# A hybrid two-layer block: the low parts of the second MLP product's weights made by an accumulating transfer

## The chip, the cores and the metric

The kernel runs on one core of one Trainium2 chip. The metric is the device time of one execution in microseconds; three runs of the kernel before gave 2245.93, 2249.05 and 2250.21, and their median, 2249.05, is the time before. A profile is one further execution.

## The reference

Two layers over 512 latent tokens and 256 context tokens, width 1024, in float32. Each layer normalizes and modulates, makes one input projection for three mixers (neighbourhood attention, a bidirectional linear recurrence, windowed attention), merges and projects them, and then runs an MLP with a squared ReLU. Only the MLP matters here:

```python
def sq_relu_mlp(h, w1, w2):
    return jnp.square(jax.nn.relu(h @ w1)) @ w2

# per layer, latent tokens; context tokens the same in layer 0
h2 = modulate(rms_norm(x, norm2_g[l]), mod_l[3], mod_l[4])
x = x + mod_l[5] * sq_relu_mlp(h2, w_ff1[l], w_ff2[l])
# at the end
return rms_norm(x, final_g)
```

`w_ff1` is 1024 x 4096 and `w_ff2` 4096 x 1024 in each layer.

## The kernel before

**Products in three passes.** Every large product is made with operands split in two float32r parts, `x = xh + xl`, `w = wh + wl`. TensorE multiplies wh by xh, wl by xh and wh by xl, in this order (`PASSES`, `gemm1`, L382), for each of the 128-row steps. So `wl` is needed at the second matmul of a weight.

**Weights.** A list `wseq` holds all weight chunks in the order of use. A chunk is 128 x 1024 float32, 512 KB. `w_load` issues its transfer from DRAM into a tile `wr` on SP's queue (L276). `w_split` then makes `wh` by a copy to float32r on ScalarE (L290) and `wl` by `raw - wh` on VectorE (L291). `w_get` hands the pair to the product; `w_ahead` writes loads and splits for some eight tiles ahead of use. All these tiles, also the raw ones and those of the modulation weights (`mw`), rotate through one pool of 12 slots (`whp`). A tile gets a slot when the last reader of an older one is done, and the instruction that first writes it waits for that.

**The MLP.** Each layer has 8 blocks of the second product. A block uses four chunks `("w2", l, n, j)`, each for two groups of 128 output rows. The first product's pairs (`("p", n)`) and the second's blocks (`("F", n)`) alternate: two pairs, then a block; the last two blocks follow each other. From pair 3 (layer 0) or 4 (layer 1) on, the first product is made with seven smaller products in place of eight (`seven`, L1507), whose weight forms `wf` are made on ScalarE (L311) and VectorE (L305 to L312) from two raw chunks. In `seven` ScalarE copies a result out of PSUM (`sv`, L1516, L1526) and VectorE adds or subtracts it (L1519, L1529, L1532) before TensorE goes on with the same PSUM tile. In layer 0 both latent and context tokens run (512 and 256 columns), and the results of the first seven blocks are scaled by ScalarE into `xo` (L1641) and added in DRAM to `xsp` by an accumulating transfer on POOL's queue (L1643), eight a block. In layer 1 only the latent tokens are left, and VectorE adds the results to `x` (L1384). During layer 0's MLP the modulation of layer 1 is made on VectorE from 48 chunks `mw` (L521, L536, L541).

**What sets the order.** The order of instructions on each engine is set when the program is built, by priorities and a scheduler's own estimate of times; `hp("ws")` shifts the priority of the split. Each engine then runs its queue strictly in that order. POOL does little: constants, 16 additions, the reciprocal square roots of the norms (L609) and the 56 transfers of L1643. Tiles are named by kind and number; `wh393` and `wl393` are the parts of the first chunk of layer 1's second-to-last block, `wh98` those of the first chunk of layer 0's second block. A number behind that (`wh393_21181`) is a count of tiles and differs between programs.

Of the kernel before, what the change touches and what calls it, by code (L numbers as in the profile page):

```python
# [8 lines left out]
F32R = mybir.dt.float32r  # L9
BF16 = mybir.dt.bfloat16  # L10
AF = mybir.ActivationFunctionType
ALU = mybir.AluOpType
# [53 lines left out]
def f(ap):  # L66
    return ap.bitcast(F32)
# [66 lines left out]
def build(tc, A, out):  # L134
    nc = tc.nc

    with ExitStack() as es:
# [46 lines left out]
        act = nc.scalar.activation  # L184

        def hp(tag):
            return tc.high_priority(HPS[tag]) if HPS.get(tag) else ExitStack()
# [41 lines left out]
        wseq = []  # L229
# [23 lines left out]
        ws = dict(load=0, split=0, use=0)  # L253
        wraw = {}
        whl = {}
        wpart = {}

        def w_tile(name, n, dt):
            return whp.tile([P, 1024], dt, tag="wh", name=f"{name}{n}")

        def w_load(i):
            while ws["load"] <= min(i, len(wseq) - 1):
                n = ws["load"]
                if wseq[n][0] == "f1":
                    _, l, p_, j = wseq[n]
                    if j == 0:
                        for c in range(2):
                            fraw[c] = w_tile("wr%d" % c, n, F32)
                            nc.sync.dma_start(fraw[c], A["w_ff1"][l, 2 * p_ + c])
                    ws["load"] += 1  # L270
                    continue
                a = A[src[wseq[n][0]]]
                for ix in wseq[n][1:]:
                    a = a[ix]
                wraw[n] = w_tile("wr", n, F32)[:, 0:a.shape[1]]
                nc.sync.dma_start(wraw[n], a)  # L276
                ws["load"] += 1

        def w_split(i):
            while ws["split"] <= min(i, len(wseq) - 1):  # L280
                n = ws["split"]
                w_load(n)
                if wseq[n][0] == "f1":
                    whl[n] = form(n, wseq[n][3])
                    ws["split"] += 1
                    continue
                r = wraw.pop(n)
                h_, l_ = (w_tile(nm, n, F32R)[:, 0:r.shape[1]] for nm in ("wh", "wl"))
                with hp("ws"):
                    act(h_, r, AF.Copy)  # L290
                    V.tensor_tensor(l_, r, f(h_), op=ALU.subtract)  # L291
                whl[n] = (h_, l_)
                ws["split"] += 1
# [4 lines left out]
        def form(n, j):  # L298

            a, b, c, d = (fraw[i // 2][:, 512 * (i % 2):512 * (i % 2) + 512] for i in range(4))  # L300
            t = w_tile("wf", n, F32R)
            with hp("ws"):
                if j == 1:
                    s1 = fraw[2] = t3("s1")[:, 0:512]
                    V.tensor_tensor(s1, c, d, op=ALU.add)  # L305
                    V.tensor_tensor(c, c, a, op=ALU.add)
                    V.tensor_tensor(a, a, s1, op=ALU.add)  # L307
                if j == 5:
                    V.tensor_tensor(b, b, a, op=ALU.add)
                r = (a, a, b, fraw.get(2), c, b, d)[j]  # L310
                act(t[:, 0:512], r, AF.Copy)  # L311
                V.tensor_tensor(t[:, 512:1024], r, f(t[:, 0:512]), op=ALU.subtract)  # L312
                if j == 3:
                    fraw.pop(2)
                if j == 6:
                    fraw.clear()
            return t
# [579 lines left out]
        for l in range(L):  # L897
# [648 lines left out]
            for it, n_ in ff_order():  # L1546
# [111 lines left out]
                a = held = None  # L1658
# [114 lines left out]
```

## Time and profile before

| what | us |
|---|---|
| median of three runs | 2249.05 |
| the profiled execution, its own time | 2246.54 |
| its span (first to last instruction) | 2244.7 |
| TensorE busy with matmuls | 2200.5 (98%) |
| VectorE busy | 1533.8 (68%) |
| ScalarE busy | 1190.4 (53%) |
| POOL busy | 91.6 (4%) |

The granted clock is 0.997 of full speed over the span. The span and 1.8 us around it make the execution's time. Matmuls overlap, so the duration of one says little; the distance between the starts of two that follow each other is what one costs. In the views, PE is TensorE, PEld its weight loads, DVE VectorE, ACT ScalarE, POOL GpSimd, SP the engine that issues most transfers; a name with q (SPq) is that engine's sequencer. L382 is line 382. Layer 0's blocks of the second product lie between 837 and 1310 us, layer 1's between 1918 and 2234 us.

### The profile page before, as it was taken

How to read it: one execution, taken by the hardware profiler on the slowest of the kernel's cores; microseconds unless marked ns; L12 is line 12 of the kernel's file. 1: busy time of each engine (PE TensorE's matmuls, PEld its weight loads, DVE VectorE, ACT ScalarE, POOL GpSimd, SP SyncE). 2: the span in 40 equal slices, each digit the busy share in tenths (PEclk: the TensorE clock that was granted, in tenths of full speed). 3: DMA queues.
4: the chain of work that ended last, by engine and by line, in shares of the span. 5: the costliest groups of instructions: out<-in, count | busy, mean ns of one | idle time of the engine just before them, and what ended most of it. 6: DMA issues, size and time to landing. Idle time of an engine off the chain costs nothing.

```text
span 2244.7 us, 35216 instructions
## 1 busy us (share of the span) xinstructions
PE 2200.5 (98%) x13617; PEld 1918.4 (85%) x13617; DVE 1533.8 (68%) x3313; ACT 1190.4 (53%) x2267; POOL 91.6 (4%) x86
## 2 busy tenths in 40 slices
PE   9999999999999999999999999999999999999998
PEld 6888888888888888998889887888878789888997
DVE  5867545677698895766666378654477777777776
ACT  4666446667532274454545446655575845444452
POOL 0000000001000001111000100000000100000000
PEclk9999999999999999999999999999999999999999
DMA  7201121112255536766776732112112232323331
GB/s 280 76 29 43 44 76 43 34 55 78 69 176 188 199 111 145 176 168 178 202 210 162 180 129 76 57 63 73 41 62 89 89 132 86 110 78 94 113 104 66
DMA packets 84502, 246.02 MB, mean 110 GB/s; under 512 B 9824, under 2 KB 13168, under 8 KB 84336
## 3 DMA queue, kind: packets, MB, share of 16 engines
q1 hardware_dynamic: 75840, 221.62, 29.5%
q0 software_dynamic: 8064, 22.02, 6.3%
q8 instruction: 107, 1.75, 0.3%
q14 instruction: 59, 0.48, 0.1%
q10 hardware_dynamic: 432, 0.14, 0.0%
HBM read 212.28 MB, written 30.42 MB: 108 GB/s over the span
## 4 chain that ended last, share of the span: by engine, by line
PE 77%; DVE 10%; ACT 7%; DMA 5%; issue 2%; POOL 0%; SPq 0%; DVEq 0%; POOLq 0%; ACTq 0%
PE gl L382 29%; PE S L382 21%; PE gc L382 5%; PE S L1507 4%; PE S L724 3%; PE O L742 3%; PE gl L1507 3%; PE gl L397 2%; DMA wr<-in_w_ff_dram 2%; PE S L672 2%; DVE wf L312 1%; PE S L673 1%; DMA mw<-in_w_mod_dram 1%; DVE wl L291 1%; PE S L397 1%
## 5 line engine op out<-in xcount | busy, mean ns | idle before, releaser
L291 DVE TENSOR_TENSOR wl<-wr,wh 128x1024 fp32r<-128x1024 f32 (+1 forms) x224 | 269.3, 1203 | 144.9 <-ACT wh L290 79.7
L290 ACT ACTIVATE wh<-wr 128x1024 fp32r<-128x1024 f32 (+1 forms) x224 | 231.6, 1038 | 93.0 <-DMA wr<-in_w_in_dram 45.7
L382 PE MATMUL gl<-hh,wh 128*128 128x512 f32 (+1 forms) x672 | 257.9, 384 | 4.7 <-DVE KL L941 2.1
L382 PE MATMUL gl<-hh,wl 128*128 128x512 f32 (+1 forms) x672 | 255.4, 380 | 0.0
L382 PE MATMUL gl<-hl,wh 128*128 128x512 f32 (+1 forms) x672 | 254.7, 379 | 0.0
L311 ACT ACTIVATE wf<-wr 128x512 fp32r<-128x512 f32 x150 | 90.2, 624 | 145.6 <-DVE wr L307 75.3
L382 PEld LDWEIGHTS gl<-hh,wh 128*128 128x128 f32 x672 | 127.0, 189 | 25.9 <-issue 5.0
L382 PEld LDWEIGHTS gl<-hl,wh 128*128 128x128 f32 x672 | 126.9, 189 | 23.8
L382 PEld LDWEIGHTS gl<-hh,wl 128*128 128x128 f32 x672 | 126.9, 189 | 18.8
L700 ACT ACTIVATE P<-S,s 128x512 f32<-128x512 f32 (+1 forms) x160 | 103.0, 647 | 70.8 <-DVE s L696 35.5
L312 DVE TENSOR_TENSOR wf<-wr,wf 128x512 fp32r<-128x512 f32 x150 | 100.9, 688 | 56.3 <-ACT wf L311 55.8
L382 PE MATMUL S<-ah,wh 128*128 128x512 f32 (+1 forms) x384 | 136.4, 355 | 0.0
L382 PE MATMUL S<-al,wh 128*128 128x512 f32 (+1 forms) x384 | 136.4, 355 | 0.0
L382 PE MATMUL S<-ah,wl 128*128 128x512 f32 (+1 forms) x384 | 136.3, 355 | 0.0
L382 PE MATMUL S<-hh,wl 128*128 128x512 f32 (+1 forms) x360 | 125.1, 348 | 1.1 <-DVE wl L291 1.1
L382 PE MATMUL gl<-ah,wl 128*128 128x512 f32 (+1 forms) x352 | 124.8, 355 | 0.2 <-DVE wl L291 0.2
L382 PE MATMUL S<-hl,wh 128*128 128x512 f32 (+1 forms) x360 | 124.7, 347 | 0.0
L382 PE MATMUL S<-hh,wh 128*128 128x512 f32 (+1 forms) x360 | 124.5, 346 | 0.2 <-ACT tau L1222 0.2
L382 PE MATMUL gl<-al,wh 128*128 128x512 f32 (+1 forms) x352 | 124.6, 354 | 0.0
L382 PE MATMUL gl<-ah,wh 128*128 128x512 f32 (+1 forms) x352 | 124.5, 354 | 0.0
L727 ACT ACTIVATE P<-S 128x512 f32<-128x512 f32 (+1 forms) x160 | 84.4, 554 | 61.6 <-PE S L724 56.7
L1507 PE MATMUL S<-hh,wf 128*128 128x384 f32 (+1 forms) x488 | 109.3, 313 | 5.4 <-ACT sv L1516 3.3
(412 smaller groups left out, 5943.7 us busy)
## 6 DMA issues: line engine op xcount, KB each, us to landing
wr<-in_w_ff_dram SPq DMA_DIRECT2D x128, 512.0 KB
wr<-in_w_in_dram SPq DMA_DIRECT2D x100, 512.0 KB
mw<-in_w_mod_dram SPq DMA_DIRECT2D x48, 512.0 KB
xsp<-xo POOLq DMA_DIRECT2D x56, 384.0 KB, 5.8
mr<-in_w_mod_dram SPq DMA_DIRECT2D x64, 256.0 KB
wr<-in_w_branch_dram SPq DMA_DIRECT2D x24, 512.0 KB
wm<-in_w_mod_dram SPq DMA_DIRECT2D x32, 256.0 KB
wr<-in_w_out_dram SPq DMA_DIRECT2D x16, 512.0 KB
```

The lines of the kernel that those rows point to most:

```text
L290: act(h_, r, AF.Copy)
L291: V.tensor_tensor(l_, r, f(h_), op=ALU.subtract)
L311: act(t[:, 0:512], r, AF.Copy)
L312: V.tensor_tensor(t[:, 512:1024], r, f(t[:, 0:512]), op=ALU.subtract)
L382: mm(o, w[wi_][:, c0 + k * P:c0 + (k + 1) * P], view(acts[k][xi]), start=(k == 0 and i == 0), stop=(k == n - 1 and i == 2))
L397: mm(os_[i], w[wi_][:, k * P:(k + 1) * P], seg.nat(acts[k][xi]), start=(k == 0 and p_ == 0), stop=(k == n - 1 and p_ == 2))
L672: mm(d, qs[:, qc:qc + P], rk, start=True, stop=False)
L700: act(p[:, 0:n0], self.S[i][:, 0:n0], AF.Exp, bias=nm[:, i:i + 1], accum_out=su[:, i:i + 1])
L724: nc.tensor.transpose(d, self.p[i][:, j * P:(j + 1) * P], ident)
L727: act(pt[:, 0:n0], self.S[i][:, 0:n0], AF.Copy)
L742: mm(o[half, oc:oc + P], vt[:, vc:vc + 64], h["pt"][:, j * P:(j + 1) * P], start=(j == 0), stop=(j == nt - 1), tile_position=(0, 64 * h["h ...
L1507: mm(o, w[:, c0:c0 + P], B[i, k][xi], start=(first and k == 0 and n == 0), stop=(last and k == 3 and n == 2), skip_group_check=True)
```

## The change

The chunks of the second product (`w2`, 64 in all) are split in another way. `w_load` takes two tiles, `wh` and `wl`, and issues a transfer on POOL's queue that goes from the float32 chunk in DRAM straight into `wh`, which is float32r: the transfer casts. `w_split` then lets ScalarE write `-wh` into `wl`, and issues a second transfer on POOL's queue that adds the float32 chunk from DRAM to `wl` (`accum_op=ALU.add`), so that `wl = raw - wh`. No raw tile is used, and no VectorE instruction. All other weights stay as they are.

```diff
@@ w_load
+                if wseq[n][0] == "w2":
+                    wraw[n] = tuple(w_tile(nm, n, F32R) for nm in ("wh", "wl"))
+                    nc.gpsimd.dma_start(wraw[n][0], a)
+                    ws["load"] += 1
+                    continue
                 wraw[n] = w_tile("wr", n, F32)[:, 0:a.shape[1]]
                 nc.sync.dma_start(wraw[n], a)
                 ws["load"] += 1
@@ w_split
+                if wseq[n][0] == "w2":
+                    h_, l_ = whl[n] = wraw.pop(n)
+                    with hp("ws"):
+                        act(l_, f(h_), AF.Copy, scale=-1.0)
+                    nc.gpsimd.dma_start(l_, A["w_ff2"][wseq[n][1:]], accum_op=ALU.add)
+                    ws["split"] += 1
+                    continue
                 r = wraw.pop(n)
```

In the changed program lines below the edit have moved on by 12 (L382 is L394, L1643 is L1655); the new transfers are L277 and L296, the negation is L295.

POOL, from the last addition into `xsp` of layer 0's first block to the first of its second block. Before, its queue holds only these additions:

```order
L1643 DMA xsp_109<-xo_1017_8821 128x768
L1643 DMA xsp_109<-xo_1020_8851 128x768
L1643 DMA xsp_109<-xo_1049_9184 128x768
L1643 DMA xsp_109<-xo_1052_9218 128x768
L1643 DMA xsp_109<-xo_1056_9263 128x768
```

Now, in the same place:

```order
L1655 DMA xsp_109<-xo_1020_8847 128x768
L277 DMA wh98_9042<-in_w_ff2_dram 128x1024
L277 DMA wh99_9077<-in_w_ff2_dram 128x1024
L296 DMA wl98_9043<-in_w_ff2_dram 128x1024
L277 DMA wh100_9109<-in_w_ff2_dram 128x1024
L296 DMA wl99_9078<-in_w_ff2_dram 128x1024
L277 DMA wh101_9157<-in_w_ff2_dram 128x1024
L296 DMA wl100_9110<-in_w_ff2_dram 128x1024
L296 DMA wl101_9158<-in_w_ff2_dram 128x1024
L1655 DMA xsp_109<-xo_1049_9176 128x768
```

Eight transfers stand between the additions of two blocks, loads and accumulations in turn, with two loads ahead of the first accumulation.

ScalarE, at the split of that block's first two chunks. Before:

```order
L642 ACTIVATE ah_1035_9017<-r_1025_8879 128x768
L1516 ACTIVATE sv_1041_9026<-S_1037_9022 128x384
L1522 ACTIVATE r_1039_9024<-S_1037_9022 128x384
L290 ACTIVATE wh98_9048<-wr98_9046 128x1024
L1526 ACTIVATE sv_1041_9026<-gl_1042_9080 128x384
L290 ACTIVATE wh99_9084<-wr99_9082 128x1024
```

Now:

```order
L654 ACTIVATE ah_1035_9013<-r_1025_8875 128x768
L1528 ACTIVATE sv_1041_9022<-S_1037_9018 128x384
L295 ACTIVATE wl98_9043<-wh98_9042 128x1024
L1534 ACTIVATE r_1039_9020<-S_1037_9018 128x384
L1538 ACTIVATE sv_1041_9022<-gl_1042_9075 128x384
L295 ACTIVATE wl99_9078<-wh99_9077 128x1024
```

The negation of chunk 98 stands one evacuation earlier than the cast did.

TensorE, at the start of layer 1's last two blocks. Before:

```order
L1507 MATMUL S_2228_21261<-q4_2036_18800,wf392_21162 128x256
L382 MATMUL gl_2233_21345<-ah_2185_20770,wh393_21181 128x512
L382 MATMUL gl_2233_21345<-ah_2185_20770,wl393_21182 128x512
L382 MATMUL gl_2233_21345<-al_2186_20771,wh393_21181 128x512
L382 MATMUL gl_2233_21345<-ah_2187_20775,wh393_21181 128x512
```

Now:

```order
L1519 MATMUL S_2228_21203<-q4_2036_18764,wf392_21106 128x256
L394 MATMUL gl_2233_21284<-ah_2185_20714,wh393_21123 128x512
L394 MATMUL S_2234_21298<-ah_2185_20714,wh393_21123 128x512
L394 MATMUL S_2235_21317<-ah_2185_20714,wh394_21171 128x512
L394 MATMUL gl_2236_21331<-ah_2185_20714,wh394_21171 128x512
L394 MATMUL gl_2233_21284<-ah_2185_20714,wl393_21124 128x512
```

The first matmuls of four output groups, all with `wh`, now stand ahead of the first one with `wl393`; the first with `wl394` is the 27th matmul of the block.

## Rows read from the trace of the kernel before

**Rows 1.** The page, part 1: busy time, share of the span and instructions by engine.
```profile
PE 2200.5 (98%) x13617; PEld 1918.4 (85%) x13617; DVE 1533.8 (68%) x3313; ACT 1190.4 (53%) x2267; POOL 91.6 (4%) x86
```

**Rows 2.** Busy time by stretch: us, then engines, granted clock, DMA share, GB/s.
```profile
949.00:1147.00 198.00, 192.03 (x1083) 176.05 (x1081) 129.23 (x272) 96.62 (x157) 20.70 (x24) 1.00 0.72 186
...
1925.00:2190.00 265.00, 263.53 (x1623) 235.04 (x1622) 186.90 (x296) 124.64 (x222) 0.00 (x0) 1.00 0.30 98
```

**Rows 3.** TensorE's waits, 820 to 1330 us: who for whom, us, times, longest.
```profile
PE gl L1507 <- DVE r L1529: 3.1, 3, 1.8
PE S L1507 <- ACT sv L1516: 2.8, 5, 1.4
PE gl L1507 <- ACT sv L1516: 1.9, 3, 0.9
PE S L1507 <- DVE r L1529: 1.5, 1, 1.5
```

**Rows 4.** The same, 1960 to 2190 us.
```profile
PE gl L1507 <- ACT sv L1516: 0.8, 2, 0.5
PE S L1507 <- ACT sv L1516: 0.5, 1, 0.5
```

**Rows 5.** The page, part 5: one group, count, busy us, mean ns, idle before.
```profile
L291 DVE TENSOR_TENSOR wl<-wr,wh 128x1024 fp32r<-128x1024 f32 (+1 forms) x224 | 269.3, 1203 | 144.9 <-ACT wh L290 79.7
```

**Rows 6.** VectorE's waits, 820 to 1330 us.
```profile
DVE wl L291 <- ACT wh L290: 43.1, 17, 10.2
DVE mw L541 <- DMA mw<-in_w_mod_dram: 18.0, 9, 4.5
...
DVE silc L536 <- DMA mw<-in_w_mod_dram: 12.0, 8, 4.4
```

**Rows 7.** POOL's accumulating transfers, by their line: ns min/median/max, landing from issue in us.
```profile
L1643 POOL DMA_DIRECT2D xsp<-xo x56: 853/862/1074, 843.4 to 1283.7; - x56
...
DMA to landing us min/median/max: 4.5/5.8/9.7
```

**Rows 8.** The page, part 3: DMA queue, packets, MB, share of 16 engines.
```profile
q1 hardware_dynamic: 75840, 221.62, 29.5%
q0 software_dynamic: 8064, 22.02, 6.3%
```

**Rows 9.** In order of time (start, us): SP, VectorE, TensorE, a block of layer 1.
```profile
1991.19 9.41 SPq L276 DMA_DIRECT2D wr<-in_w_ff_dram  x4
...
1996.62 1.23 DVE L291 TENSOR_TENSOR wl<-wr,wh 128x1024 fp32r<-128x1024 f32 x1 [0.78 <-ACT wh L290]
...
2004.65 0.40 PE L382 MATMUL S<-ah,wl 128*128 128x512 f32 x1
```

**Rows 10.** The same of layer 0's second block, with ScalarE.
```profile
887.94 8.33 SPq L276 DMA_DIRECT2D wr<-in_w_ff_dram  x3
...
892.97 0.47 ACT L1516 ACTIVATE sv<-S 128x384 f32<-128x384 f32 x1
...
897.37 1.23 DVE L291 TENSOR_TENSOR wl<-wr,wh 128x1024 fp32r<-128x1024 f32 x1 [0.17 <-ACT wh L290]
...
903.28 0.39 PE L382 MATMUL gl<-ah,wl 128*128 128x512 f32 x1
```

**Rows 11.** The same of layer 0's tightest later block.
```profile
1154.68 1.23 DVE L291 TENSOR_TENSOR wl<-wr,wh 128x1024 fp32r<-128x1024 f32 x1
...
1165.42 0.39 PE L382 MATMUL gl<-ah,wl 128*128 128x512 f32 x1
```

**Rows 12.** The same of the last two blocks, ScalarE and TensorE.
```profile
2181.83 1.05 ACT L290 ACTIVATE wh<-wr 128x1024 fp32r<-128x1024 f32 x1
...
2187.08 1.04 ACT L290 ACTIVATE wh<-wr 128x1024 fp32r<-128x1024 f32 x1
...
2185.62 0.40 PE L382 MATMUL gl<-ah,wh 128*128 128x512 f32 x1
2185.85 0.40 PE L382 MATMUL gl<-ah,wl 128*128 128x512 f32 x1
```

## The prediction

> **What bounds the kernel now.** I read the busy shares first, then the stretches of the two MLPs, then who waits for whom there, and last single transfers and weights in order of time. TensorE is busy for 2200.5 of 2244.7 us [rows 1]: the time is TensorE's stream of matmuls plus its few gaps. In three cycles of layer 0's MLP (949 to 1147 us) it is busy 192.0 of 198 us, and in layer 1's MLP (1925 to 2190) 263.5 of 265 [rows 2]. So there is little to win where the change acts. In layer 0's whole stretch with second-product blocks, TensorE's four longest kinds of wait sum to 3.1 + 2.8 + 1.9 + 1.5 = 9.3 us, all in front of the first product's matmuls (L1507), behind an evacuation that VectorE or ScalarE makes late [rows 3]; in layer 1 they are 1.3 us [rows 4]. The second product (L382 with `ah`, `al`) appears in none of these rows: its weights are always there in time. What they are worth is therefore how early each `wl` is there, and that slack is what the change spends.
>
> **What the change removes.** Of the 224 subtractions on VectorE (L291), 64 go, at 1203 ns mean [rows 5], so 77 us, half in each layer; each wide one takes 1.23 us. ScalarE keeps one pass per weight, of the same shape (the negation for the cast). SP loses 64 loads, and the slots of the raw chunks go: a weight takes two slots of the weight pool instead of three while it is made. In layer 0's stretch VectorE also stood still for 43.1 us, 17 times, behind ScalarE's cast [rows 6]; most of these were second-product weights. None of this is TensorE time by itself. It can only shorten the waits of [rows 3], of which the two on L1529 (3.1 + 1.5 = 4.6 us) name VectorE. I take back 1 us of them: the rest hangs on ScalarE's order, which keeps every pass, and on the loads of `mw` and of the first product, which stay. The bounds are 0 and all 9.3.
>
> **What it adds: two transfers per weight on POOL's queue.** No transfer of the trace casts, and none accumulates into SBUF; the nearest rows are the 56 accumulations `xsp<-xo` of 384 KB into DRAM. POOL spends 853 to 1074 ns on issuing one, and it lands 4.5, 5.8 (median) and 9.7 us after that begins [rows 7]. Their packets hold the 16 engines for 6.3% of 2244.7 = 141 us [rows 8], 2.53 us each; a 512 KB one would take 3.37, so 0.84 more. An accumulation of 512 KB then lands in 5.3, 6.6 or 10.5 us. The medians come from the stretch where the DMA engines are 72% busy; in layer 1 they are 30% busy [rows 2], and there I take 6.0, between the minimum and the median. A plain 512 KB load holds the engines 29.5% of the span / 221.62 MB x 0.524 MB = 1.57 us [rows 8]. So a casting load lands in 6.6 - 3.37 + 1.57 = 4.8 us if it moves like a plain one (my choice: the word size stays the same, and no second operand is read) and in 6.6 if it moves at the pace of an accumulation.
>
> All of that is one chain for a weight: load, negation (1.05 us), accumulation. Behind a cast, `wl` is ready after 1.07 + 1.23 us today and would be after 1.05 + 6.0. POOL takes them in order, two loads ahead of the first accumulation; an accumulation that waits for its negation holds back the next load behind it, and in layer 0 the eight `xsp<-xo`, which nobody waits for until the layer's end. Behind the last accumulation stands the power of the final norm (L609), which needs sums that TensorE makes after using that weight, so it isn't held. ScalarE's negation waits for its load, as the cast does today, with first-product evacuations queued behind it; in the block of [rows 9] it would end at 1997.05, where the cast ended at 1996.6, so it holds them 0.4 us longer. TensorE waits at the second matmul of a weight (the one with `wl`). So I go through the first weight of each block, where the slack is least:
> - Layer 0, second block. Load at 887.94. It lands at 892.7; ScalarE's order now puts the negation right behind the copy of 892.97, so it runs from 893.4 to 894.5, where today's subtraction ends only at 897.37 + 1.23 = 898.6. The accumulation lands at 894.5 + 6.6 = 901.1; TensorE wants it at 903.28 [rows 10]: 2.2 us to spare, nothing lost. At 10.5 it is 1.7 late.
> - Layer 0, the other blocks. The tightest has its subtraction at 1154.68 and its matmul at 1165.42 [rows 11]: 1154.7 + 6.6 = 1161.3, 4 us to spare, and no stall even at 10.5.
> - Layer 1, the four equal blocks. Load at 1991.19, landed at 1996.0, negated at 1997.05, accumulated at 2003.05; wanted at 2004.65 [rows 9]. The slack of today (2004.65 - 1997.85 = 6.8 us) shrinks to 1.6. At 6.6 it is 1.0; at 8 each block would lose 0.4.
> - The last two blocks. Here ScalarE comes to the first weight at 2181.83, since it stands behind an evacuation that waits for TensorE, however early the load is. Negated at 2182.9, accumulated at 2188.9. TensorE reaches it at 2185.62 [rows 12]; its new order puts four matmuls with `wh` first, each 0.23 us [rows 12], which gives 2186.55. It stands still for **2.4 us**. The second weight, negated from 2187.08 [rows 12], lands at 2194.1 and is wanted 26 matmuls after 2185.62, at 2191.7, so with the 2.4 us just in time. The rest of this stretch is two transfers a weight, some 5 us of the engines, against 5.6 us of matmuls, and starts with the loads ahead. By the bounds 5.3, 6.6 and 10.5 the stall is 1.7, 3.0 and 6.9; it is nothing only if the accumulation lands in 3.6 us, and no row is that short.
>
> For this price the Trainium skill has a rule ("DMA: Bandwidth & Descriptors", section "Anatomy of one DMA — SWDGE (gpsimd) path"): a transfer issued by GpSimd takes about 2.0 us plus bytes over 436e3. It would give 3.2 us for this accumulation, and the stall of 2.4 would be nothing. The trace speaks against it: by the same rule the 384 KB accumulation is 2.9, and it took 5.8 [rows 7].
>
> DMA room: each of layer 0's cycles is 66 us (three in 198) at 72% [rows 2], that is 47.5 us; four accumulations of 3.37 make it 61.0, or 92%. It fits, with longer landings, which fall on the loads of `mw`: VectorE already stands still behind these for 18.0 + 12.0 us [rows 6]. I let them cost nothing on TensorE, since 39 us of subtractions and the 43.1 us of waiting leave the same queue.
>
> The sum against the profiled execution: 2246.54 + 2.4 - 1 = 2247.9. That execution is 2.5 us under the median of the runs, so **2250.4 us** on the median of 2249.05. This is the same time: a measurement of this kernel can tell about 0.2%, or 4.5 us.
>
> **Rivals.**
> - *The DMA engines fill up in layer 0* (slower). If the casting loads move at the accumulation's pace, four of them add 4 x 1.80 = 7.2 us to each cycle: 68.2 us of engine time in 66, 103%. Six cycles get 2.2 us longer, 13 us; with a tail of 3.0 that is 2249.05 + 16 = 2265. It decides at a casting load that holds the engines over some 2.8 us. For it: the only software transfers of the trace hold an engine 2.1 times as long per byte [rows 8]. Against: these read two operands, a cast reads one.
> - *The waits of layer 0 go* (faster). VectorE gets free and ScalarE with it. With 8 of the 9.3 us gone and a tail of 1.7: 2249.05 - 6.3 = 2242.7. For it: VectorE's queue loses 82 us there. Against: ScalarE is named for as many of these waits as VectorE, and its queue keeps its length.
> - *POOL can't issue when VectorE is busy* (slower). Should POOL's issues be held for one VectorE instruction each (1.2 us), a load and an accumulation come 2.4 us later: 0.8 in each of four blocks of layer 1, and 2.4 + 1.2 at the end, 2249.05 + 6.8 = 2255.9. Against: 56 issues beside a busy VectorE took 853 to 1074 ns [rows 7]. The Trainium skill states this as a rule ("SBUF — State Buffer", section "SBUF: two separate sides"): a VectorE instruction in a two-port mode keeps GpSimd from writing descriptors. By it the time would be the 2256 of this rival.
> - *Late only at the end* (slower): a landing of 10.5 us in the last blocks, 6.9 - 1, gives 2254.9.
> - *Accumulations land in 3.6 us*: no tail, 2248; the same time.
>
> **How the numbers follow.** Forecast 0.50 (its own range 2247.5 to 2252.5), quick landing 0.04: the same, 0.54. DMA engines full 0.20, POOL held 0.07, late at the end 0.06: slower by over 0.2%, 0.33. Waits gone 0.13: faster by over 0.2%. The range takes in the waits gone at its lower end and the full engines at its upper: 2243 to 2267, with about 0.06 left out below it and 0.12 above.
>
> **What would show it.** Right: 64 accumulations that land in 5.5 to 7 us in layer 1; TensorE with a wait of 1.7 to 3.0 us on the DMA of a `wl` shortly after 2185 and no other wait on `wl`; VectorE busy about 77 us less. A DMA share near 0.9 in layer 0's cycles, and TensorE's waits at L1507 near 9 us. Wrong: waits on `wl` in the equal blocks of layer 1 (landings over 7.6), a layer 0 that gets longer by more than 5 us (engines full), casting loads whose packets take twice a plain one's, or POOL issues far over 0.9 us.

## The result: 33 us slower, far outside the range

The changed kernel takes 2281.0 us (median; 2272.9 to 2283.9) against 2247.5 of the kernel before in the same runs: a ratio of 1.0142, with a 95% interval of 1.0122 to 1.0163. The prediction was 2250.4 us, with a range that ended at 2267. The profiled execution's span is 2278.0 us.

The page of the changed kernel has these lines (part 1, part 3, and one group of part 5; they answer to [rows 1, 5, 8]):

```profile
PE 2211.7 (97%) x13617; PEld 1926.4 (85%) x13617; DVE 1461.3 (64%) x3249; ACT 1189.3 (52%) x2267; POOL 183.2 (8%) x214
...
q1 hardware_dynamic: 66624, 188.06, 24.3%
q0 software_dynamic: 26496, 89.14, 18.8%
...
L295 ACT ACTIVATE wl<-wh 128x1024 fp32r<-128x1024 f32 x64 | 67.7, 1057 | 118.2 <-DMA wh<-in_w_ff_dram 116.4
```

VectorE lost 72.5 us of work, as meant. TensorE runs the same 13617 matmuls and is busy 11 us longer with them, so some ran slowly, and it is idle for 22 us more. To see where, I divided both executions at the same matmuls: the first matmul of layer 0's first second-product block, of its last two blocks, of their last weight, of layer 1's first block, of its last two blocks and of their last weight. Views of busy time by stretch, columns as in [rows 2]; the kernel before, then the changed one:

```profile
837.31:1245.28 407.97, 397.34 (x2246) 366.64 (x2245) 265.33 (x544) 201.22 (x330) 41.58 (x48) 1.00 0.68 176
1245.28:1295.45 50.17, 50.17 (x265) 42.88 (x265) 15.31 (x18) 21.57 (x33) 6.91 (x8) 1.00 0.74 178
1295.45:1918.29 622.84, 613.17 (x3813) 521.26 (x3812) 431.63 (x934) 376.43 (x730) 20.12 (x12) 1.00 0.25 82
1918.29:2185.62 267.33, 265.86 (x1634) 236.94 (x1633) 190.65 (x305) 124.86 (x225) 0.00 (x0) 1.00 0.31 99
2185.62:2216.45 30.83, 30.83 (x170) 26.54 (x169) 18.67 (x26) 11.64 (x17) 0.00 (x0) 1.00 0.20 70
```

```profile
836.20:1249.88 413.68, 399.56 (x2246) 369.92 (x2245) 237.76 (x518) 200.70 (x330) 75.54 (x96) 0.99 0.82 200
1249.88:1308.39 58.51, 53.72 (x265) 44.91 (x265) 7.92 (x11) 20.38 (x32) 12.98 (x16) 0.94 0.89 208
1308.39:1933.27 624.88, 614.27 (x3813) 521.43 (x3812) 430.58 (x937) 377.52 (x733) 25.06 (x19) 1.00 0.26 83
1933.27:2214.86 281.59, 269.66 (x1634) 239.80 (x1633) 164.44 (x279) 124.65 (x224) 31.88 (x45) 0.99 0.51 132
2214.86:2249.63 34.77, 32.70 (x170) 27.65 (x169) 11.60 (x20) 11.80 (x17) 8.80 (x12) 0.95 0.93 209
```

The numbers of matmuls agree row by row, so the lengths can be subtracted: 5.7 us are lost in layer 0's blocks up to the last two, 8.3 in the last two, 2.0 between the layers, **14.3 in layer 1's equal blocks**, 3.9 in its last two blocks. The prediction had 2.4 in the last stretch, and 1 less in layer 0's blocks.

Two things make up the large losses. In layer 1's equal blocks TensorE is idle for 281.59 - 269.66 = 11.9 us where it was idle for 1.5, and the same 1634 matmuls take 3.8 us longer. The second part is the clock. One of the gaps, by stretch:

```profile
2047.35:2050.64 3.29, 0.04 (x1) 0.00 (x0) 3.13 (x6) 1.46 (x4) 0.00 (x0) 1.00 0.00 0
2050.64:2054.06 3.42, 3.41 (x16) 3.41 (x17) 2.72 (x5) 1.44 (x4) 0.00 (x0) 0.50 0.00 0
2054.06:2057.48 3.42, 3.42 (x31) 3.42 (x31) 1.91 (x4) 1.36 (x3) 0.81 (x2) 1.00 0.17 42
```

After 3.3 us in which TensorE did nothing the granted clock is 0.50 of full speed (1.2 instead of 2.4 GHz) for 3.4 us, and 16 matmuls run where the next 3.4 us have 31. In the stretches above the clock fell like this after six gaps, for 23.9 us in all; in the four stretches that hold these falls, matmuls got 11.4 us longer in all (in the one between the layers, which holds none, 1.1). (The Trainium skill, "TensorE: Matmul & The Clock Gate", section "HAM oscillation — how this bites in real kernels", prices throttled time at one half of it: an estimate of 12.0 us here, and the trace agrees.) The kernel before has a clock of 1.00 in every one of these rows.

Who TensorE waited for in layer 1's equal blocks, which answers to [rows 4] (us, times, longest):

```profile
PE gl L1519 <- ACT sv L1528: 6.2, 5, 3.3
PE S L1519 <- ACT sv L1528: 3.7, 3, 1.8
PE gl L1519 <- ACT sv L1538: 1.9, 1, 1.9
```

No wait is for a `wl`. All are in front of the *first* product, behind an evacuation by ScalarE, and sum to 11.8 us (L1519 and L1528 are L1507 and L1516 of before).

### The profile page after: what moved, and what is told of

It reads as the page before. It is cut to its first block, busy times and chain, and to the rows that moved or that the text cites. A ratio compares the mean times of both kernels' runs of the same rounds, so it can differ in the third digit from the quotient of the medians.

```text
span 2278.0 us, 35473 instructions
## 1 busy us (share of the span) xinstructions
PE 2211.7 (97%) x13617; PEld 1926.4 (85%) x13617; DVE 1461.3 (64%) x3249; ACT 1189.3 (52%) x2267; POOL 183.2 (8%) x214
## 4 chain that ended last, share of the span: by engine, by line
PE 54%; issue 17%; DVE 10%; DMA 9%; ACT 6%; POOL 3%; SPq 0%; POOLq 0%; DVEq 0%; ACTq 0%
PE gl L394 21%; PE S L394 13%; PE gc L394 4%; DMA wh<-in_w_ff_dram 3%; PE S L736 3%; PE O L754 3%; PE gl L409 2%; DMA wr<-in_w_ff_dram 2%; PE S L684 2%; PE S L1519 1%; DMA wr<-in_w_in_dram 1%; PE S L685 1%; DVE wl L303 1%; DMA mw<-in_w_mod_dram 1%; POOL xsp L1655 1%
## 5 line engine op out<-in xcount | busy, mean ns | idle before, releaser
L303 DVE TENSOR_TENSOR wl<-wr,wh 128x1024 fp32r<-128x1024 f32 (+1 forms) x160 | 190.9, 1194 | 121.2 <-ACT wh L302 56.2
L394 PE MATMUL gl<-hh,wh 128*128 128x512 f32 (+1 forms) x672 | 257.4, 383 | 4.7 <-DVE KL L953 2.1
L394 PE MATMUL gl<-hh,wl 128*128 128x512 f32 (+1 forms) x672 | 254.9, 379 | 0.0
L394 PE MATMUL gl<-hl,wh 128*128 128x512 f32 (+1 forms) x672 | 254.3, 378 | 0.0
L302 ACT ACTIVATE wh<-wr 128x1024 fp32r<-128x1024 f32 (+1 forms) x160 | 164.8, 1033 | 84.4 <-DMA wr<-in_w_in_dram 51.4
L394 PEld LDWEIGHTS gl<-hh,wh 128*128 128x128 f32 x672 | 126.5, 188 | 25.8 <-issue 5.0
L324 DVE TENSOR_TENSOR wf<-wr,wf 128x512 fp32r<-128x512 f32 x150 | 100.9, 688 | 72.0 <-ACT wf L323 70.9
L394 PEld LDWEIGHTS gl<-hl,wh 128*128 128x128 f32 x672 | 126.6, 188 | 23.6
L394 PEld LDWEIGHTS gl<-hh,wl 128*128 128x128 f32 x672 | 126.7, 188 | 18.7
L394 PE MATMUL S<-ah,wl 128*128 128x512 f32 (+1 forms) x384 | 136.5, 355 | 0.0
L394 PE MATMUL S<-al,wh 128*128 128x512 f32 (+1 forms) x384 | 136.3, 355 | 0.0
L394 PE MATMUL S<-ah,wh 128*128 128x512 f32 (+1 forms) x384 | 136.1, 355 | 0.0
L394 PE MATMUL gl<-ah,wh 128*128 128x512 f32 (+1 forms) x352 | 126.4, 359 | 4.8 <-ACT xo L1653 4.3
L295 ACT ACTIVATE wl<-wh 128x1024 fp32r<-128x1024 f32 x64 | 67.7, 1057 | 118.2 <-DMA wh<-in_w_ff_dram 116.4
L394 PE MATMUL gl<-ah,wl 128*128 128x512 f32 (+1 forms) x352 | 127.0, 361 | 2.3 <-DMA wl<-in_w_ff_dram 2.3
L394 PE MATMUL gl<-al,wh 128*128 128x512 f32 (+1 forms) x352 | 126.2, 358 | 0.0
L394 PE MATMUL S<-hh,wl 128*128 128x512 f32 (+1 forms) x360 | 125.0, 348 | 1.1 <-DVE wl L303 1.1
L394 PE MATMUL S<-hh,wh 128*128 128x512 f32 (+1 forms) x360 | 124.5, 346 | 0.2 <-ACT tau L1234 0.2
L394 PE MATMUL S<-hl,wh 128*128 128x512 f32 (+1 forms) x360 | 124.6, 347 | 0.0
L1519 PE MATMUL S<-hh,wf 128*128 128x384 f32 (+1 forms) x488 | 110.8, 317 | 11.9 <-ACT sv L1528 9.3
```

The lines of the kernel that those rows point to most:

```text
L295: act(l_, f(h_), AF.Copy, scale=-1.0)
L394: mm(o, w[wi_][:, c0 + k * P:c0 + (k + 1) * P], view(acts[k][xi]), start=(k == 0 and i == 0), stop=(k == n - 1 and i == 2))
L1519: mm(o, w[:, c0:c0 + P], B[i, k][xi], start=(first and k == 0 and n == 0), stop=(last and k == 3 and n == 2), skip_group_check=True)
```

## Where the late evacuation comes from

ScalarE's timeline at one such gap: the same place of layer 1 before, then after (start, us, line, operation, in brackets the idle time ahead of it and what ended it).

```profile
2024.89 0.63 ACT L311 ACTIVATE wf<-wr 128x512 fp32r<-128x512 f32 x1 [1.91 <-DMA wr<-in_w_ff_dram]
2028.41 0.38 ACT L1516 ACTIVATE sv<-gl 128x256 f32<-128x256 f32 x1 [2.88 <-PE gl L1507]
2030.58 0.63 ACT L311 ACTIVATE wf<-wr 128x512 fp32r<-128x512 f32 x1 [1.78 <-DVE wr L307]
```

```profile
2027.40 1.06 ACT L295 ACTIVATE wl<-wh 128x1024 fp32r<-128x1024 f32 x1 [4.30 <-DMA wh<-in_w_ff_dram]
...
2030.60 0.61 ACT L323 ACTIVATE wf<-wr 128x512 fp32r<-128x512 f32 x1
...
2045.02 0.63 ACT L323 ACTIVATE wf<-wr 128x512 fp32r<-128x512 f32 x1 [4.56 <-DMA wr<-in_w_ff_dram]
2049.18 1.15 ACT L323 ACTIVATE wf<-wr 128x512 fp32r<-128x512 f32 x2 [3.52 <-DVE wr L319]
2050.23 0.36 ACT L1528 ACTIVATE sv<-gl 128x256 f32<-128x256 f32 x1
```

`wf` are the seven weights that are formed from a pair of raw chunks (`wr`) of the first product; `sv` is the evacuation for which TensorE's next product waits. Before, `sv` stands right behind the first forming pass, and ScalarE waits there for TensorE (2.88 us): it is early. After, two more forming passes stand ahead of `sv`, and these wait 3.5 us for VectorE's sums of the chunks. The program's own order, ScalarE's rows around it, shows that this was planned so, and not only happened (before, then changed):

```
1898 L311 ACTIVATE wf_19644<-wr_19640 128x512
1899 L1516 ACTIVATE sv_19679<-gl_19675 128x256
1900 L311 ACTIVATE wf_19680<-wr_19640 128x512

1897 L323 ACTIVATE wf_19600<-wr_19596 128x512
1898 L323 ACTIVATE wf_19636<-wr_19596 128x512
1899 L323 ACTIVATE wf_19656<-wr_19596 128x512
1900 L1528 ACTIVATE sv_19635<-gl_19631 128x256
```

Four of TensorE's nine waits in the equal blocks stand behind these two passes: 3.3, 0.5, 1.3 and 1.8 us, 6.7 of the 11.8, and both falls of the clock follow such a gap. The other five, 5.1 us, stand behind a negation: in four of them the new order puts it directly ahead of the evacuation, and in one, 1.9 us, it stands where a cast stood before and waits for its casting load.

So there were two suspects, and the experiments are about them: transfers that come late (ScalarE stands for 4.3 us before the negation of 2027.40 and for 4.6 us before the raw chunk's pass at 2045.02), and an order that hands lateness on.

These two waits are links of one chain. The raw chunk of 2045.02 was issued at 2041.21 and landed within 3.8 us, so its own transfer wasn't slow. It was issued late: SyncE waited for a slot that a pass of VectorE on the pair before it (`wf`, L324, 2040.49 to 2041.18) set free. The passes on that pair began at 2030.60, when ScalarE came to them behind the negation of 2027.40, whose casting load had taken 10.3 us (issued at 2017.12, landed at 2027.38). In the four cycles with such a gap these passes began 8.5, 5.9, 6.7 and 7.0 us after the block's first matmul, and TensorE then stood for 3.3, 0.5, 1.3 and 1.8 us, each time 5.2 to 5.5 us less.

## Experiments

**The two layers apart.** The condition on `"w2"` gets the layer as a second term (`== 0` in the first kernel, `== 1` in the other).

```diff
-                if wseq[n][0] == "w2":
+                if wseq[n][0] == "w2" and wseq[n][1] == 0:
```

> Only layer 0's second-product weights go through the casting load and the accumulation; layer 1 is as before. In the changed kernel TensorE is 15.0 us later than before when layer 1's first second-product block begins, and 18.2 us more are lost from there to the end. If the two layers' losses don't depend on each other: 2247.5 + 15 = 2262, and layer 1 shows no wait of TensorE longer than before. If layer 1's loss is handed on from layer 0 (a transfer or an order that came late and stays late), this one stays near 2275.

> Only layer 1's weights go through the transfers. Independent losses: 2247.5 + 18 = 2266. Theory ORDER (the plan of the changed program puts the second pair's raw loads of the first product some 2 us later, and an evacuation of ScalarE behind the passes that wait for them) and theory QUEUE (the casting loads stand in POOL's queue behind accumulations, land up to 11 us late, and ScalarE stands before them with evacuations behind) both give this. DMA engines that are full in layer 0 would put all of the loss into layer 0, and give 2250 here.

Measured: 2265.9 us (ratio 1.0101, 1.0068 to 1.0134) and 2265.1 us (1.0084, 1.0068 to 1.0100). Layer 1's loss is its own and needs nothing from layer 0: 15.4 us are lost in its equal blocks in the second kernel, none in the first. Together the two ratios make more (1.85%) than both layers at once (1.42%).

**Without the accumulation, and with a copy in its place.** The first kernel has no line here, the second a plain copy.

```diff
-                    nc.gpsimd.dma_start(l_, A["w_ff2"][wseq[n][1:]], accum_op=ALU.add)
+                    nc.gpsimd.dma_start(l_, A["w_ff2"][wseq[n][1:]])
```

> The accumulating transfers are left out, so the low part is minus the high part alone: the casting load and the negation stay. QUEUE: the casting loads land in 4 to 5 us instead of 6.2 (11 at most), ScalarE's standing still before them falls from 116 us to under 40, TensorE's gaps behind a negation (1.9, 0.8, 0.7, 1.2 us in layer 1, 2.0 in layer 0) and the stall of 2.1 us in the last two blocks go. ORDER: the gaps behind the raw loads of the first product (3.3, 0.5, 1.3, 1.8 us in layer 1, 2.4 and 1.7 in layer 0, and the half clock after four of them) stay, since nothing of the order on SP and ScalarE hangs on the accumulation. Both true: about 2265. QUEUE alone: 2250. ORDER alone: 2277.

> The accumulating transfers become plain copies of the same chunk by the same queue, with the same waits and with every engine's order unchanged, so the low part holds the raw chunk and not the difference. Only the time on the DMA engines changes: a 4 KB packet of a plain transfer took about 0.17 us in the changed kernel's trace, one of an accumulation 0.33, so 1.3 us of the engines for each weight instead of 2.65. Theory BURST (four loads and four accumulations, 16 us of all DMA engines, are asked for within some 20 us; what is asked for in that time, the later casting loads, the first product's raw chunks, `mw`, lands late, and ScalarE's fixed order hands it to TensorE): most of the loss goes, 2260 or less. Theory QUEUE (POOL takes the transfers in order, and an accumulation that waits for its negation holds the next load back): the waits are the same, so 2275 or more.

Measured: 2253.6 us (1.0020, 1.0006 to 1.0033) and 2262.7 us (1.0058, 1.0038 to 1.0077). With every engine's order as in the changed kernel (in no_acc TensorE's and VectorE's differ in layer 1's last two blocks), a copy instead of an addition takes away 18 of the 33 us, and leaving the transfer out takes away 27. So the accumulations' time on the DMA engines is one factor; the changed order alone loses 1.8 us in layer 1's equal blocks (no_acc, same stretches as above), where the passes on the first pair begin 3.4 us after a block's first matmul, and not 5.9 to 8.5. ORDER alone falls by no_acc, which it put at 2277, QUEUE alone by the copy, which it put at 2275 or more; BURST's 2260 for the copy was missed by 2.7. The trace tells why an addition weighs twice: of the 16,384 packets of 4 KB on POOL's queue in the changed kernel 7,266 took 0.16 to 0.18 us (a plain load's: 0.159, median) and 7,054 took 0.32 to 0.34.

**Who stands before the late loads.** Three kernels take ScalarE out of the way: all four casting loads of a block ahead of its first accumulation, the negation on GpSimd, the negation on VectorE. One added line each, in this order, of which the last two stand for the line taken out; in the first, `wl` is also taken from the pool only at the negation, and no longer at the load.

```diff
+                    w_load(n + 3 - wseq[n][3])
-                        act(l_, f(h_), AF.Copy, scale=-1.0)
+                        nc.gpsimd.tensor_scalar(l_, f(h_), -1.0, None, op0=ALU.mult)
+                        V.tensor_scalar(l_, f(h_), -1.0, None, op0=ALU.mult)
```

> All four casting loads of a block are issued ahead of its first negation and accumulation, so that none of them stands behind an accumulation in POOL's queue. QUEUE: landings of the casting loads at most 7 us, ScalarE's standing before them from 116 to some 50 us, and 8 to 10 us less in all, 2272. DMA engines as the cause: the four loads now share the engines with each other, the landings stay at 6 to 11 us, and the time at 2281. ORDER: the gaps behind the raw loads of the first product stay where they are, or move with the new plan.

> The negation runs on GpSimd, between its own casting load and accumulation, and ScalarE has nothing to do with these weights. Theory SCALAR (the time is lost because ScalarE stands before late casting loads with evacuations behind it, 116 us): the standing is gone, and so is most of the loss, 2258 or less. BURST: the accumulations still fill the DMA engines and delay the first product's raw chunks, for which ScalarE's forming passes wait: 2270 or more, with a longer stall in the last two blocks, where the chain of a weight gets longer by about 2 us (2.2 us for 128x768 on GpSimd in the trace).

> The negation runs on VectorE instead of ScalarE; all transfers stay. SCALAR: ScalarE doesn't stand before the casting loads any more, so the evacuations come in time, and VectorE, with 77 us less of subtractions and some 40 to 77 us of negations, carries the standing: under 2265. BURST: the first product's raw chunks land as late as before, and VectorE stands with the additions into `x` behind it: 2275 or more.

Measured: 2295.5 us (1.0218, 1.0184 to 1.0253), 2364.2 us (1.0504, 1.0476 to 1.0532) and 2280.3 us (1.0146, 1.0119 to 1.0174). In loads_first ScalarE stood before the casting loads for 3.7 us instead of 116, and the kernel got slower still: the raw chunks of the first product now came behind four accumulations at once. Its equal blocks of layer 1 lose 22.5 us, and 16.8 of TensorE's 17.2 us of idle time there are five gaps of 2.9 to 4.1 us, each behind the two forming passes. So ScalarE's standing before `wh`, 116 us in 46 times, isn't what the loss needs: theory SCALAR falls. In the changed kernel this standing is one way in which lateness gets to the forming passes; here the raw chunks bring it. neg_vec is no better than the changed kernel in the sum, but it settles less: VectorE now stands before the casting loads, for 118.5 us, and 6.3 of TensorE's 9.0 idle us in the equal blocks are waits for VectorE's results (L1541). neg_pool doesn't tell the theories apart, since it made a new bound, GpSimd itself. Its group of negations, and TensorE's waits from 1965 us on:

```profile
L295 POOL TENSOR_SCALAR wl<-wh 128x1024 fp32r<-128x1024 f32 x64 | 194.5, 3039 | 236.5 <-DMA wh<-in_w_ff_dram 128.0 <-issue 42.5 <-PE gl L394 15.7
```

```profile
PE S L394 <- DMA wl<-in_w_ff_dram: 23.9, 14, 3.7
PE gl L394 <- DMA wl<-in_w_ff_dram: 23.0, 7, 9.2
```

Load, negation (3.0 us) and accumulation take turns in one queue, one weight at a time, and here the `wl` are late.

**The casting load alone.** A raw chunk on SyncE's queue as well, the subtraction on VectorE as before.

```diff
-                    wraw[n] = tuple(w_tile(nm, n, F32R) for nm in ("wh", "wl"))
+                    wraw[n] = w_tile("wh", n, F32R), w_tile("wr", n, F32)
                     nc.gpsimd.dma_start(wraw[n][0], a)
+                    nc.sync.dma_start(wraw[n][1], a)
```

> The high part comes by the casting load, the raw chunk by a plain load of its own on SyncE's queue, and VectorE subtracts as before: no accumulation, no negation, ScalarE loses the 64 casts (67 us), and a weight is loaded twice, at 1.3 + 1.3 us of the DMA engines instead of 1.3. BURST: little is lost, 2248 to 2254. A casting load that costs by itself (its queue, its landing): 2260. If ScalarE's passes were what the waits of layer 0 hung on, this gains: 2242.

Measured: 2249.2 us (1.0002, 0.9992 to 1.0011). The casting load costs nothing, though each weight is loaded twice; and 64 passes less on ScalarE gain nothing.

**Half the weights, and all but the last blocks.** Again a second term, one for each kernel.

```diff
+                if wseq[n][0] == "w2" and wseq[n][3] % 2 == 0:
+                if wseq[n][0] == "w2" and wseq[n][2] < NFF - 2:
```

> Only two of the four weights of a block go by transfers (the first and the third), the others are split as before. BURST: 8 us of the DMA engines a block instead of 16 leave room for the other loads, so the loss falls by much more than half, 2255. If each transfer costs by itself (its issue, its landing, its negation), the loss is half: 2264.

> The last two blocks of either layer are split as before, all others by transfers. From the changed kernel's trace against before: the stretch from the first matmul of the last two blocks on costs some 8 us in layer 0 and 4 us in layer 1 (of which 2.1 is the stall on `wl`). If these belong to those blocks alone, 2281 - 12 = 2269. If the loss in layer 0's last blocks comes from something that was late earlier, 2275 or more.

Measured: 2264.1 us (1.0060, 1.0037 to 1.0084) and 2272.1 us (1.0101, 1.0063 to 1.0139). By the sum, half is a miss for BURST: it loses some 42% of the loss, not much less than half. By stretches it isn't one thing: its equal blocks of layer 1 lose 0.1 us, and its end of layer 0 and its last two blocks lose 4.1 and 5.1. keep_last loses 1.0 us at the end of layer 0 and nothing in the last two blocks, so what is lost there belongs to those blocks.

**The accumulations beside the kernel before, and in its chain.** The first kernel adds the first of these lines to the kernel before, for each second-product weight, into eight spare tiles in DRAM; the second keeps that kernel's raw loads and ScalarE's casts, and has the other two lines in the place of its subtraction.

```diff
+                    nc.gpsimd.dma_start(spare[k % 8], f(h_), **(dict(accum_op=ALU.add) if k >= 8 else {}))

-                    V.tensor_tensor(l_, r, f(h_), op=ALU.subtract)
+                        V.tensor_scalar(l_, f(h_), -1.0, None, op0=ALU.mult)
+                    nc.gpsimd.dma_start(l_, A["w_ff2"][wseq[n][1:]], accum_op=ALU.add)
```

> The kernel before, with 64 more transfers beside it on GpSimd's queue: each adds a second-product weight's high part (512 KB) into a spare buffer in DRAM, one for each weight, issued when the high part is there; no instruction waits for one but the next owner of the weight's buffer. So the DMA engines carry the accumulations of the changed kernel and none of its chain, its negation or its casting loads. BURST in its plain form (the engines' time alone makes the loss): 2260 to 2275. If the lost time needs the changed order as well (ScalarE's negation standing before a load, the raw chunks of the first product asked for later, an evacuation placed behind passes that wait for them), the kernel before has slack for late loads: within 4 us of 2248.

> Raw chunks come by SyncE's queue and are cast by ScalarE as before; the low part is the negation (on VectorE) to which the accumulating transfer adds the raw chunk. So the accumulations are those of the changed kernel and lie in each weight's chain, but no casting load stands in GpSimd's queue, a weight takes three buffers again, and the order of ScalarE in layer 1 is that of the kernel before (the first evacuation of a second pair stands ahead of the passes that wait for VectorE). Theory ORDER x BURST (late raw chunks cost TensorE time only where the evacuation stands behind them): layer 1's equal blocks lose at most 3 us; what is left is the end of layer 0 (8 to 10 us, as with the accumulations beside the kernel before) and the stall of the last two blocks (2 to 6): 2262 to 2266. If the accumulation in the chain is what costs, wherever the evacuation stands: 2275 or more.

Measured: 2260.6 us (1.0053, 1.0035 to 1.0071) and 2287.4 us (1.0170, 1.0149 to 1.0191). before_plus_acc was the run that surprised most. Its stretches (end of layer 0, equal blocks of layer 1), and ScalarE's waits for raw chunks in the second:

```profile
1241.52:1301.62 60.10, 52.00 (x265) 43.96 (x265) 16.07 (x18) 21.21 (x33) 11.22 (x13) 0.94 0.87 204
1925.06:2192.61 267.55, 266.23 (x1634) 237.04 (x1632) 190.30 (x305) 125.82 (x225) 18.94 (x22) 1.00 0.53 141
```

```profile
ACT wf L317 <- DMA wr<-in_w_ff_dram: 19.4, 11, 3.4
```

The DMA share in layer 1's equal blocks is that of the changed kernel (0.53 against 0.51), and they take 267.55 us against 267.33: full engines alone cost nothing there. The raw chunks are late there too (ScalarE stands before them for 19.4 us, 5.8 in the kernel before), but the evacuations stand where they stood, and nothing is lost. The loss of the profiled execution is the end of layer 0, 9.9 us; it took 2253.6 us, 7 under the median, and where the other executions lose these 7 isn't known. acc_only, with the evacuation behind one forming pass as before in all cycles of layer 1 but the first, loses 5.3 us in the equal blocks, of which TensorE's waits on `wl` are 4.3 (1.6, 1.0 and 1.7 us), so the part that I forecast at 3 held only without these; but the end of layer 0 (11.2) and above all the last two blocks (12.1) cost more than the 8 to 10 and 2 to 6 that I gave, and the sum was missed by 21 us.

**The order alone, all transfers kept.** One tile less of weights is made ahead, from layer 0's last block on. In the program the evacuation then stands behind one forming pass again; the edit also moves the negations of layer 1's blocks from just ahead of an evacuation to other places, and some raw chunks wait for other slots.

```diff
-                    wroom[0] = 2 * WA
+                    wroom[0] = 2 * WA - 1
```

> The changed kernel with one tile less of weights made ahead from the end of layer 0 on (7 instead of 8). All transfers stay; in layer 1's blocks ScalarE's first evacuation of a second pair comes to stand ahead of the forming passes that wait for VectorE, where the kernel before has it. ORDER x BURST: the equal blocks of layer 1, which cost 14 us, cost 4 at most, and TensorE's gaps of 3.3 and 1.8 us behind the evacuation with the half clock after them go: 2270. If the place of the evacuation has no part in it: 2280, or more, since the casting loads are asked for later too.

> The control for the run above: the kernel before with the same 7 tiles ahead instead of 8. It is to show what one tile less is worth by itself: within 3 us of 2248 if the weights have slack, as their landings say; if it gains or loses more than that, the run above is to be read against it.

> Both at once: 7 tiles ahead, and the last two blocks of either layer split as before. If the three causes add up (the place of the evacuation in layer 1's blocks some 10 us, the end of layer 0 some 8, the last two blocks 4), little but layer 0's cycles is left: 2252 to 2259. If layer 0's cycles take it back, 2265 or more.

Measured: 2265.0 us (1.0094, 1.0071 to 1.0117), 2246.3 us (0.9995, 0.9985 to 1.0006) and 2255.6 us (1.0038, 1.0023 to 1.0053). The line itself is worth nothing to the kernel before, and 16 us to the changed one. order_back in layer 1's equal blocks (by stretch), and its casting loads (who waited for them, and their landing):

```profile
1932.04:2197.74 265.70, 264.90 (x1634) 236.40 (x1632) 162.96 (x278) 123.11 (x223) 31.96 (x45) 1.00 0.54 140
```

```profile
  ACT wl L295: 125.7, 43
...
DMA to landing us min/median/max: 3.7/6.3/11.8
```

The casting loads are as late as they were, ScalarE stands before them even longer (125.7 us), and 14.3 us of loss are gone: TensorE is idle for 0.8 us in 265.7. ScalarE there:

```profile
2040.20 0.63 ACT L323 ACTIVATE wf<-wr 128x512 fp32r<-128x512 f32 x1 [1.50 <-DVE wf L324]
2042.35 0.39 ACT L1528 ACTIVATE sv<-gl 128x256 f32<-128x256 f32 x1 [1.52 <-PE gl L1519]
2044.56 1.15 ACT L323 ACTIVATE wf<-wr 128x512 fp32r<-128x512 f32 x2 [1.82 <-DVE wr L319]
```

`sv` waits for TensorE again (1.52 us), and not TensorE for `sv`. The two passes behind it still wait for VectorE, and end at 2045.71, 3.4 us after `sv` began: by these rows an evacuation behind them would have come about that much later. Measured from each block's first matmul in these four cycles, the passes on the first pair begin 8.5 to 9.0 us later (5.9 to 8.5 in the changed kernel) and the two passes on the second pair 25.4 to 26.0 us later (24.2 to 27.0), so the passes are as late as there. The evacuation comes at 23.8 us, as in the kernel before (23.8 to 24.0), and at 25.3 to 28.1 in the changed kernel. With the last blocks as before, too, 8.7 us are left, 8.5 of them in layer 0's first six blocks. Apart, the two edits took away 16 and 9 us, together 25, though the 9 is loose (keep_last ran from 2264 to 2282). By stretches they are separate causes: order_back still loses 8.4 us at the end of layer 0 and 3.8 in the last two blocks, and keep_last still loses 10.7 in the equal blocks. No kernel of the study beats the kernel before.

## The end of layer 0

Beside the order, the other large item is here: 8.3 us, with one idle gap of 4.27 us and 6.8 us at half the clock. Timeline of the changed kernel, POOL, SP, ScalarE and TensorE:

```profile
1259.13 0.86 POOL L296 DMA_DIRECT2D wl<-in_w_ff_dram  x1 [0.21 <-issue]
1259.68 0.87 POOL L277 DMA_DIRECT2D wh<-in_w_ff_dram  x1
1260.23 1.21 POOL L1655 DMA_DIRECT2D xsp<-xo  x1
1269.58 0.87 POOL L296 DMA_DIRECT2D wl<-in_w_ff_dram  x1 [8.14 <-ACT wl L295]
1270.52 0.87 POOL L1655 DMA_DIRECT2D xsp<-xo  x1
...
1282.43 0.38 SPq L281 DMA_DIRECT2D wr<-in_w_in_dram  x1
...
1290.92 1.06 ACT L302 ACTIVATE wh<-wr 128x1024 fp32r<-128x1024 f32 x1 [7.86 <-DMA wr<-in_w_in_dram]
1291.88 1.04 ACT L1653 ACTIVATE xo<-S,modT 128x512 f32<-128x512 f32 x2
...
1293.55 0.80 PE L394 MATMUL gl<-ah,wh 128*128 128x512 f32 x1 [4.27 <-ACT xo L1653]
```

POOL stands 8.14 us before an accumulation whose negation waits for its load, with an addition `xsp<-xo` behind it. SyncE reads these sums back (`x<-xsp`) and has layer 1's first weight behind that in its queue. That weight is asked for 32.6 us after the stretch began (28.9 before: 1274.22 - 1245.28, from SyncE's timeline of the kernel before), lands after 8.5 us (7.2 before) among transfers that keep the engines 89% busy, and ScalarE stands 7.86 us before its cast (6.21 before) with the evacuations `xo` behind it. That accumulations make this loss is shown: it is 0.2 us in no_acc, 1.0 in keep_last, 9.9 in before_plus_acc. Which of the two, the place in POOL's queue or the engines' time, weighs more is open: a copy instead of the addition still loses 3.7 (in a profiled execution 7 us under its median).

## The prediction, step by step

- **The subtractions.** VectorE's 72.5 us less (77 forecast). The 1 us that I took back from layer 0's waits didn't come: these waits (L1519 on ScalarE and VectorE, 820 to 1330 us) are 14.1 us instead of 10.6 (9.3 in the four kinds of [rows 3]).
- **The transfers' own times.** The views of the two lines, with POOL's issue in ns and the landing in us:

```profile
L277 POOL DMA_DIRECT2D wh<-in_w_ff_dram x64: 543/572/897, 811.6 to 2235.7; - x64
...
DMA to landing us min/median/max: 3.7/6.2/11.0
```

```profile
L296 POOL DMA_DIRECT2D wl<-in_w_ff_dram x64: 858/874/910, 817.1 to 2244.8; - x64
...
DMA to landing us min/median/max: 5.2/6.9/9.8
```

  The accumulation was forecast at 5.3, 6.6 and 10.5: right (in layer 1's equal blocks, where I took 6.0, the median is 6.9). It holds the engines for less than I had: 128 packets of 0.33 us on 16 engines make 2.6 us, not 3.37, and layer 0's blocks are at 0.82, under the 92% that I had. The rule of the Trainium skill that I set against it ("DMA: Bandwidth & Descriptors", section "Anatomy of one DMA — SWDGE (gpsimd) path") gives an estimate of 3.2 us, and the shortest of 64 took 5.2. The casting load's pace was right as well (its packets take a plain load's time), but it lands in 6.2 and up to 11.0 us, where I had 4.8: I had priced it by itself, and in the bursts it shares the engines with accumulations. POOL's issues are as short as ever, so the rival in which VectorE holds them falls.
- **The slack of `wl`.** Right in outcome in every place. In layer 1's equal blocks no `wl` is late (11.8 us of waits, none of them on it); the first one of a block landed 2.6 to 8.1 us ahead of its matmul, where I had 1.6. In the last two blocks TensorE has four matmuls with `wh` and then stands for 2.07 us, where I had 2.4:

```profile
2214.86 0.40 PE L394 MATMUL gl<-ah,wh 128*128 128x512 f32 x1
2215.09 0.63 PE L394 MATMUL S<-ah,wh 128*128 128x512 f32 x2
2215.56 0.39 PE L394 MATMUL gl<-ah,wh 128*128 128x512 f32 x1
2218.02 0.80 PE L394 MATMUL gl<-ah,wl 128*128 128x512 f32 x1 [2.07 <-DMA wl<-in_w_ff_dram]
```

  What I left out is the clock: half speed after the gap makes 3.9 us of it.
- **The step that failed** is the one after that: "I go through the first weight of each block, where the slack is least", and, for all else, "it holds them 0.4 us longer" and "I let them cost nothing on TensorE". I asked where the *new* operations would be late, found the one place, and took the rest of the program's order as it had been. But the program's order is made anew for each program, and it had moved an evacuation that was 2.9 us early behind two passes that wait for raw chunks, and four negations to just ahead of other evacuations; the bursts made casting loads late, and these, by way of ScalarE and the slots, the raw chunks. The "0.4 us longer" that a negation was to hold ScalarE was 2.4 to 4.3 us at the last weight of each block, which I didn't go through. The average DMA share of layer 1 (0.51) hid the bursts. Either factor alone costs 2 us or less in these blocks (no_acc 1.8, before_plus_acc 0.2); both cost 14.3, and with the order back it is nothing. Of the 14.3 the two passes make some 10 (6.7 us of waits, and the two falls of the clock, some 3.4), an estimate from the gaps above; the negations make most of the rest. Nothing in the trace of before could have shown the new order; the built program could, three rows of ScalarE's.
- **The end of layer 0.** "The eight `xsp<-xo`, which nobody waits for until the layer's end" was true, and the layer's end was then not priced. It is the second failed step, 8.3 us.
- **The rival "DMA engines fill up in layer 0"** has the nearest time (2265), and by the wrong way: it needed casting loads at an accumulation's pace. The share in layer 0's blocks rose to 0.82, and 5.7 us were lost there. No run explains them: 5.2 are lost there in no_acc too, where nothing is added to a `wl`. How much of these belong to the change is open: this stretch differs by -3.6 us in the profiled execution of layer1_only, where its work is as before, and by +21.6 in keep_last, whose profiled execution is 9.8 us over its median.

## What to carry to other kernels

When a change adds transfers, price them at whoever shares the DMA engines and the queues with them, in the stretch in which they are issued, and not by their own landing and an average share. Then read the new program's order at every instruction that stands between TensorE and its next product: an evacuation that comes to stand behind a pass that waits for a load turns lateness that was free into idle time. And a gap of TensorE can cost more than itself: six here, of 1.8 to 4.3 us, were followed by 3.4 us or more at half the clock, some 1.7 us or more on top of each.

## What the runs showed of the hardware

An accumulating packet of 4 KB holds a DMA engine for 0.33 us and a casting one for 0.17, about as long as a plain one (0.16). Landings of 128x1024 transfers stretched to two or three times their shortest (3.7 to 11.0 us, 5.2 to 9.8 us) where four loads and four accumulations were issued within some 20 us. GpSimd needs 3.04 us for a negation of 128x1024 float32, ScalarE 1.06. The clock fell to one half after gaps of 1.8 to 4.3 us that followed on long stretches at full speed, but not after every gap of that size: after one of 1.9 us at 1975.8 it stayed at full speed.
